# Block kernels of a state-space layer: eight 128 KB loads in place of sixteen 64 KB loads, for three of four blocks

## The chip, the cores and the metric

The kernel runs on one core of a Trainium2 chip. The metric is the device time of one execution in microseconds (us). Three runs of the kernel before are shown, and their median counts. One further execution was profiled; its trace is what all readings below come from.

## The reference

Two decoder layers over 512 positions of width 1024. The first layer mixes tokens with a diagonal complex state-space model (64 groups of 16 channels, 64 states each), followed by a GELU, a gated linear unit and an output projection; the second with stick-breaking attention. Each is followed by a layer norm and a dense SwiGLU network with its own norm. The change lies in the state-space mixer alone:

```python
mag = jnp.exp(lam_re * dt)
lbar_re = mag * jnp.cos(lam_im * dt)
lbar_im = mag * jnp.sin(lam_im * dt)
...
_, _, s_re, s_im = lax.associative_scan(
    _ssm_combine, (a_seq_re, a_seq_im, bu_re, bu_im), axis=0)
y = (jnp.einsum('lbgp,ghp->blgh', s_re, c_re.astype(f32))
     - jnp.einsum('lbgp,ghp->blgh', s_im, c_im.astype(f32)))
y = y.reshape(bsz, seq, D_MODEL) + d_skip.astype(f32) * x.astype(f32)
h = jax.nn.gelu(y).astype(x.dtype)
```

## The kernel before

The scan is not run position by position. The 512 positions are cut into 64 chunks of 8. Inside a chunk the output is a small convolution of the chunk's inputs with a kernel of lags (the intra-chunk kernel); between chunks only the states are scanned, and their effect is added. The 64 groups are handled in four blocks of 16 groups (numbered 0 to 3).

For each block the order of the work is written out by hand in `SSM_ORDER`, a string of words of one letter and a block number (or a count): `g`, `j` and `h`, `i` build tables on DVE; `t`, `T`, `m`, `M` transpose and multiply on PE; `k` (function `p_k`) computes the intra-chunk kernels on PE, ACT copies them to SBUF (L887), and two transfers of 128 KB write them to a DRAM scratch `kd` (L888); `n` (`f_n`) loads them back in another layout (L901); `r` and `s` scan the states on DVE; `y` (`p_y`, L969) is the product that needs the loaded kernels and the states; `z` transposes its result and applies the GELU; `u` is a piece of the gated linear unit on PE, `p` and `q` split a weight into two parts, `d` are products whose result isn't used. This whole stage runs under a manual schedule of all five engines, so each engine and the queues of SP and ACT execute in exactly this order.

The round trip through DRAM is needed because `p_y` wants, for each group, a 128 by 128 matrix in which partition n*16+h holds row h of the kernel shifted by n positions: the loads read `kd` eight times with overlapping windows, one load for each n, and so write 16 partitions each. In the kernel before each n is loaded twice, for groups 0 to 7 and for groups 8 to 15 of the block. The target is `tn`, two halves of 1024 columns. Blocks 0, 1 and 2 put it into idle parts of `xl` and `xh` (table `TNX`), where the two halves lie side by side, so the profile names those loads `xl<-kd` and `xh<-kd`; block 3 takes two separate tiles (`tn<-kd`). All loads are issued by SP, save the second half of block 0, which ACT issues.

`p_y` goes through 8 steps j; in each, for two groups, one product with `tn` and two with the states. Steps 0 to 3 read the first half of `tn` and steps 4 to 7 the second.

Every transfer signals one of eight completion semaphores in turn (`DMAHW0` to `DMAHW7`), so the issue of a transfer waits until the one eight places before it has landed.

Of the kernel before, what the change touches and what calls it, by code (L numbers as in the profile page):

```python
# [22 lines left out]
L = 8  # L23
# [286 lines left out]
class Trunk:  # L310
# [341 lines left out]
    def ssm(self):  # L652


        tc, nc, io, ring, ws = self.tc, self.nc, self.io, self.ring, self.ws
# [27 lines left out]
        half = lambda t, i: t[:, i * NG * L:(i + 1) * NG * L].rearrange("p (a g n) -> p a g n", a=2, n=4)  # L683
# [24 lines left out]
        for hf in range(4):  # L708
# [4 lines left out]
        kd = dr.tile([NBLK, 16, 32, 240], F32, name="kd")  # L713
# [4 lines left out]
                          in_=zero.unsqueeze(1).to_broadcast([128, NBLK * 4, 112]))  # L718
# [172 lines left out]
            ring.put(ksb)  # L891

        def f_n(b):
            if b in TNX:
                half = (self.xl, self.xh)[TNX[b]][:, 4:8].rearrange("p k t -> p (k t)").bitcast(F32)
                tn = [half[:, :1024], half[:, 1024:]]
            else:
                tn = [ring.get("tn", F32) for _ in range(2)]
            for hf in range(2):
                for n in range(L):  # L900
                    (nc.scalar if b == 0 and hf else nc.sync).dma_start(  # L901
                        out=tn[hf][n * 16:(n + 1) * 16].rearrange("p (g t) -> p g t", g=8),
                        in_=kd[b, hf * 8:hf * 8 + 8, 0:16, n * 16:n * 16 + 128].rearrange("g h t -> h g t"))
            st[b]["tn"] = tn

        def f_e(b):
# [87 lines left out]
        def f_l(b, e=V):  # L994
            tt(self.xl[:, 2 * b:2 * b + 2], st[b]["hg2"], self.xh[:, 2 * b:2 * b + 2].bitcast(F32), SUB, e)
            ring.put(st[b]["hg"])
# [61 lines left out]
        def pump(e):  # L1058
# [4 lines left out]
        fs = dict(c=a_c, g=f_g, j=lambda b: f_g(b, 1), h=f_h, i=lambda b: f_h(b, 1), d=p_d, t=p_t,  # L1063
                  T=lambda b: p_t(b, 1), m=p_m, M=lambda b: p_m(b, 1), e=f_e, k=p_k, r=f_r, y=p_y, l=f_l,
                  L=lambda b: f_l(b, G_), n=f_n, s=f_s, z=p_z,
                  B=lambda b: (powers(rest_), G_.memset(scr[0][:, 0:1], 0.0), scr_done()), b=lambda b: (levels(rest_), scr_done()))
        ET = mybir.EngineType
# [376 lines left out]
```

## Time and profile before

| | |
|---|---|
| runs | 1207.26, 1207.07, 1202.6 us; median 1207.07 us |
| profiled execution | 1201.96 us, span 1200.2 us |
| loads of blocks 0, 1, 2, 3, first issue | 34.78, 71.76, 97.92, 125.13 us |
| busy in the span: PE, DVE, ACT, POOL | 96%, 74%, 43%, 32% |
| data moved | 117.91 MB |

Times in the rows are microseconds from the start of the span. PE multiplies (PEld loads its weights), DVE, ACT and POOL are the elementwise engines, SPq and ACTq the issue of transfers on SP and ACT. "To landing" is the time from a transfer's issue to its completion signal. A row of the timeline gives start, duration, engine, line, operation, and in brackets the idle time before it and what ended it. A row by windows gives for each engine the busy time, then PE's granted clock, the busy share of the 16 DMA engines, and GB/s.

### The profile page before, as it was taken

The numbers are of one execution on the slowest core, as the hardware profiler recorded it, in microseconds if no ns is written. First come the engines' busy times: TensorE is split into PE (matmuls) and PEld (weight loads), VectorE is DVE, ScalarE is ACT, GpSimd is POOL, SyncE is SP. The second block draws the span as 40 slices with busy tenths as digits, with TensorE's granted clock in tenths as the row PEclk, the third lists the DMA queues.
The fourth block names the chain that finished last, engine by engine and source line by source line (L and its number), as shares of the span: only waits on it lengthen the run. The fifth ranks groups of instructions, "written<-read, shape, count | busy, mean of one in ns | idle before, by whom it ended". The sixth has DMA issues, their size and how long they took to land.

```text
span 1200.2 us, 20813 instructions
## 1 busy us (share of the span) xinstructions
PE 1156.9 (96%) x8494; PEld 1035.8 (86%) x8494; DVE 894.0 (74%) x1406; ACT 512.5 (43%) x813; POOL 378.6 (32%) x333
## 2 busy tenths in 40 slices
PE   3899999999999999999999999999999999999996
PEld 3777788899999999888887888878999999998885
DVE  8888585798788777435867787877987778884446
ACT  1355273054444445331156665653444444454300
POOL 6644402036455551001312322221254556510000
PEclk9999999999999999999999999999999999999999
DMA  5433741023323325431201121221233232264201
GB/s 199 115 81 81 233 168 47 1 89 108 122 87 121 109 90 197 137 110 66 106 13 59 54 71 53 72 88 53 89 106 123 72 123 90 88 227 141 70 18 52
DMA packets 44799, 117.91 MB, mean 98 GB/s; under 512 B 6816, under 2 KB 18080, under 8 KB 44576
## 3 DMA queue, kind: packets, MB, share of 16 engines
q1 hardware_dynamic: 43552, 116.07, 28.9%
q8 instruction: 66, 1.08, 0.4%
q10 hardware_dynamic: 1152, 0.52, 0.3%
q14 instruction: 29, 0.24, 0.1%
HBM read 112.51 MB, written 4.06 MB: 97 GB/s over the span
## 4 chain that ended last, share of the span: by engine, by line
PE 83%; DVE 10%; ACT 2%; issue 2%; POOL 2%; DMA 1%; SPq 0%; DVEq 0%; POOLq 0%; ACTq 0%
PE psum L359 16%; PE psum L361 16%; PE psum L360 16%; PE psum L378 8%; PE psum L380 8%; PE psum L379 8%; PE psum L969 2%; DVE nb L1212 1%; PE psum L1234 1%; ACT wh L290 1%; DVE wl L295 1%; PE psum L1299 1%; PE psum L1250 1%; POOL be L1213 1%; PE psum L1249 1%
## 5 line engine op out<-in xcount | busy, mean ns | idle before, releaser
L233 POOL TENSOR_TENSOR wf<-raw,wf 128x1024 fp32r<-128x1024 f32 (+1 forms) x80 | 160.0, 2015 | 128.5 <-ACT wf L246 81.6
L360 PE MATMUL psum<-xf,wf 128*128 128x256 f32 x640 | 181.4, 283 | 0.6 <-DVE wf L233 0.6
L361 PE MATMUL psum<-xf,wf 128*128 128x256 f32 x640 | 181.7, 284 | 0.0
L359 PE MATMUL psum<-xf,wf 128*128 128x256 f32 x640 | 181.5, 284 | 0.0
L295 DVE TENSOR_TENSOR wl<-raw,wh 128x1024 fp32r<-128x1024 f32 x91 | 119.6, 1325 | 59.1 <-ACT wh L290 40.3
L359 PE MATMUL psum<-xh,wh 128*128 128x512 f32 (+1 forms) x416 | 146.0, 352 | 1.8 <-ACT xh L992 1.3
L290 ACT ACTIVATE wh<-raw 128x1024 fp32r<-128x1024 f32 x108 | 112.4, 1054 | 76.1 <-PE psum L380 25.9
L361 PE MATMUL psum<-xl,wh 128*128 128x512 f32 (+1 forms) x416 | 141.4, 343 | 0.5 <-DVE xl L658 0.5
L360 PE MATMUL psum<-xh,wl 128*128 128x512 f32 (+1 forms) x416 | 141.1, 340 | 0.3 <-POOL wl L295 0.3
L380 PE MATMUL psum<-wh,hid 128*128 128x512 f32 x352 | 137.8, 392 | 0.0
L379 PE MATMUL psum<-wl,hid 128*128 128x512 f32 x352 | 137.5, 391 | 0.0
L378 PE MATMUL psum<-wh,hid 128*128 128x512 f32 x352 | 137.4, 390 | 0.0
L359 PE MATMUL psum<-xh,wf 128*128 128x256 f32 x480 | 134.9, 281 | 0.1
L361 PE MATMUL psum<-xl,wf 128*128 128x256 f32 x480 | 134.1, 279 | 0.0
L360 PE MATMUL psum<-xh,wf 128*128 128x256 f32 x480 | 134.1, 279 | 0.0
L360 PEld LDWEIGHTS psum<-xf,wf 128*128 128x128 f32 x640 | 122.3, 191 | 0.8 <-DVE wf L233 0.8
L359 PEld LDWEIGHTS psum<-xf,wf 128*128 128x128 f32 x640 | 122.6, 192 | 0.0
L361 PEld LDWEIGHTS psum<-xf,wf 128*128 128x128 f32 x640 | 122.3, 191 | 0.0
L295 POOL TENSOR_TENSOR wl<-raw,wh 128x1024 fp32r<-128x1024 f32 x17 | 41.9, 2476 | 177.0 <-DVE wl L295 96.6
L462 DVE TENSOR_TENSOR cv<-cv,psum 128x512 f32<-128x512 f32 x80 | 54.6, 683 | 48.6 <-PE psum L361 39.6
L359 PEld LDWEIGHTS psum<-xh,wf 128*128 128x128 f32 x480 | 90.5, 188 | 0.3 <-DVE hid L597 0.3
L361 PEld LDWEIGHTS psum<-xl,wf 128*128 128x128 f32 x480 | 90.3, 188 | 0.0
(227 smaller groups left out, 2679.2 us busy)
## 6 DMA issues: line engine op xcount, KB each, us to landing
raw<-w_gu SPq DMA_DIRECT2D x88, 512.0 KB, 3.4
raw<-w_down SPq DMA_DIRECT2D x44, 512.0 KB, 3.9
raw<-w_glu SPq DMA_DIRECT2D x16, 512.0 KB, 5.0
raw<-w_qk SPq DMA_DIRECT2D x16, 512.0 KB, 3.3
raw<-w_out SPq DMA_DIRECT2D x8, 512.0 KB, 3.4
raw<-w_v SPq DMA_DIRECT2D x8, 512.0 KB, 3.5
raw<-w_o SPq DMA_DIRECT2D x8, 512.0 KB, 3.2
xres<-xs SPq DMA_DIRECT2D x4, 512.0 KB, 6.9
```

The lines of the kernel that those rows point to most:

```text
L233: tt = lambda o, a, b, op=SUB, e=V: e.tensor_tensor(out=o, in0=a, in1=b, op=op)
L290: nc.scalar.activation(h, w, AF.Copy)
L295: (self.l_eng or nc.vector).tensor_tensor(out=l, in0=w, in1=h.bitcast(F32), op=SUB)
L359: mm(out=out, lhsT=sh, rhs=mh, start=first, stop=False)
L360: mm(out=out, lhsT=sl, rhs=mh, start=False, stop=False)
L361: mm(out=out, lhsT=sh, rhs=ml, start=False, stop=last)
L378: mm(out=o, lhsT=sh[:, ts], rhs=hl[0][:, c], start=first, stop=False)
L379: mm(out=o, lhsT=sh[:, ts], rhs=hl[1][:, c], start=False, stop=False)
L380: mm(out=o, lhsT=sl[:, ts], rhs=hl[0][:, c], start=False, stop=last)
L462: tt = lambda o, a, b, op=ADD: V.tensor_tensor(out=o, in0=a, in1=b, op=op)
L969: nc.tensor.matmul(out=yp[rows, j], lhsT=a, rhs=m_, start=step == 0, stop=step == 2)
L1212: V.tensor_tensor_scan(nb[:, h], nb[:, h], dm[u], 0.0, MUL, ADD)
```

## The change

For blocks 0, 1 and 2 one load for each n now brings all 16 groups, 16 by 16 by 128 elements (128 KB) where it was 16 by 8 by 128 (64 KB). The bytes, the 512-byte runs that they are read in, and the addresses that they go to are the same. In block 0 ACT issues the odd n and SP the even ones; before, ACT issued the second half of the groups. Block 3 keeps its 16 loads of 64 KB. The code around it moves down by four lines (L969 becomes L973), and nothing else differs.

```diff
         def f_n(b):
+
+            lags = lambda gs, n: kd[b, gs, 0:16, n * 16:n * 16 + 128].rearrange("g h t -> h g t")
             if b in TNX:
                 half = (self.xl, self.xh)[TNX[b]][:, 4:8].rearrange("p k t -> p (k t)").bitcast(F32)
                 tn = [half[:, :1024], half[:, 1024:]]
+                for n in range(L):
+                    (nc.scalar if b == 0 and n % 2 else nc.sync).dma_start(
+                        out=half[n * 16:(n + 1) * 16].rearrange("p (g t) -> p g t", g=16), in_=lags(slice(0, 16), n))
             else:
                 tn = [ring.get("tn", F32) for _ in range(2)]
-            for hf in range(2):
-                for n in range(L):
-                    (nc.scalar if b == 0 and hf else nc.sync).dma_start(
-                        out=tn[hf][n * 16:(n + 1) * 16].rearrange("p (g t) -> p g t", g=8),
-                        in_=kd[b, hf * 8:hf * 8 + 8, 0:16, n * 16:n * 16 + 128].rearrange("g h t -> h g t"))
+                for hf in range(2):
+                    for n in range(L):
+                        nc.sync.dma_start(out=tn[hf][n * 16:(n + 1) * 16].rearrange("p (g t) -> p g t", g=8),
+                                          in_=lags(slice(hf * 8, hf * 8 + 8), n))
             st[b]["tn"] = tn
```

What it does to the waits is seen in SP's queue at block 1. Before, the two writes of the kernels to `kd` stand ahead of the loads; the first load waits for the first write (`DMAHW2`), and the loads wait one after another for those eight places ahead:

```order
L888 DMA kd<-ksb_754 128x2x128 [waits DMAHW2_49,Activation_49]
L888 DMA kd<-ksb_754 128x2x128 [waits DMAHW3_49,Activation_49]
L901 DMA xh<-kd 16x8x128 [waits DMAHW4_49,DMAHW2_49]
L901 DMA xh<-kd 16x8x128 [waits DMAHW5_49]
L901 DMA xh<-kd 16x8x128 [waits DMAHW6_49]
L901 DMA xh<-kd 16x8x128 [waits DMAHW7_49]
L901 DMA xh<-kd 16x8x128 [waits DMAHW0_49]
L901 DMA xh<-kd 16x8x128 [waits DMAHW1_49]
L901 DMA xh<-kd 16x8x128
L901 DMA xh<-kd 16x8x128 [waits DMAHW3_49]
```

(eight more loads follow). With the change:

```order
L888 DMA kd<-ksb_746 128x2x128 [waits DMAHW2_49,Activation_49]
L888 DMA kd<-ksb_746 128x2x128 [waits DMAHW3_49,Activation_49]
L900 DMA xh<-kd 16x16x128 [waits DMAHW4_49,DMAHW3_49,DMAHW2_49]
L900 DMA xh<-kd 16x16x128 [waits DMAHW5_49]
L900 DMA xh<-kd 16x16x128 [waits DMAHW6_49]
L900 DMA xh<-kd 16x16x128 [waits DMAHW7_49]
L900 DMA xh<-kd 16x16x128 [waits DMAHW0_49]
L900 DMA xh<-kd 16x16x128 [waits DMAHW1_49]
L900 DMA xh<-kd 16x16x128 x2
L226 DMA raw_843<-w_glu 128x1024 [waits DMAHW4_49,PE_49]
```

The first load now waits for both writes (`DMAHW2` and `DMAHW3`), and no load waits for another load of its block.

On PE, at the middle of block 1's `p_y` (from the end of step 2 to step 4), the kernel before waits for the eight loads of the second half:

```order
L969 MATMUL psum<-h_736,s_923 64x128 x2
L969 MATMUL psum<-xh,xres 64x128 x2
L969 MATMUL psum<-h_701,s_923 64x128 x2
L969 MATMUL psum<-h_736,s_923 64x128 x2
L969 MATMUL psum<-xh,xres 64x128 [waits DMAHW4_49,DMAHW3_49,DMAHW5_49,DMAHW2_49,DMAHW6_49,DMAHW1_49,DMAHW7_49,DMAHW0_49,Activation_49]
```

With the change only a wait for ACT is left there, and the first product of `p_y` waits for all eight loads of the block, so for both halves:

```order
L973 MATMUL psum<-h_728,s_907 64x128 x2
L973 MATMUL psum<-xh,xres 64x128 x2
L973 MATMUL psum<-h_693,s_907 64x128 x2
L973 MATMUL psum<-h_728,s_907 64x128 x2
L973 MATMUL psum<-xh,xres 64x128 [waits Activation_49]
```

## The prediction

> **What bounds the kernel now.** I read the page first: the busy shares and the shares of the chain that ended last.
>
> ```profile
> PE 1156.9 (96%) x8494; PEld 1035.8 (86%) x8494; DVE 894.0 (74%) x1406; ACT 512.5 (43%) x813; POOL 378.6 (32%) x333
> PE 83%; DVE 10%; ACT 2%; issue 2%; POOL 2%; DMA 1%; SPq 0%; DVEq 0%; POOLq 0%; ACTq 0%
> ```
>
> PE bounds the whole, and DMA holds 1% of the chain. So a load is worth something only where PE stands still for it, or where a later load would make PE stand still. Next come PE's waits up to 180 us, where the loads of the four blocks lie (total, times, longest).
>
> ```profile
> PE psum L969 <- DMA tn<-kd: 1.4, 1, 1.4
> PE psum L969 <- DMA xl<-kd: 1.2, 1, 1.2
> PE psum L969 <- issue: 0.2, 1, 0.2
> ```
>
> Two waits for these loads exist: 1.4 us for `tn` in block 3, which the change leaves as it is, and 1.2 us for `xl`. The timeline of SP and ACT shows the loads of blocks 0, 1 and 2 (start, duration), that of PE the products that use them.
>
> ```profile
> 32.84 0.89 SPq L888 DMA_DIRECT2D kd<-ksb  x2
> 34.78 5.44 SPq L901 DMA_DIRECT2D xl<-kd  x8
> 35.29 6.17 ACTq L901 DMA_DIRECT2D xl<-kd  x8
> 69.06 1.78 SPq L888 DMA_DIRECT2D kd<-ksb  x2
> 71.76 7.42 SPq L901 DMA_DIRECT2D xh<-kd  x16
> 95.00 1.75 SPq L888 DMA_DIRECT2D kd<-ksb  x2
> 97.92 7.67 SPq L901 DMA_DIRECT2D xl<-kd  x16
> ```
>
> ```profile
> 43.80 0.44 PE L969 MATMUL psum<-xl,xres 128*64 128x128 f32 x4 [1.15 <-DMA xl<-kd]
> 52.89 1.06 PE L834 MATMUL psum<-ident,g 128*128 128x128 f32 x8 [0.37 <-DVE g L658]
> 53.79 1.04 PE L984 MATMUL psum<-ident,ysb 128*128 128x128 f32 x8
> 77.78 0.44 PE L969 MATMUL psum<-xh,xres 128*64 128x128 f32 x4 [0.18 <-issue]
> 81.67 0.44 PE L969 MATMUL psum<-xh,xres 128*64 128x128 f32 x4
> 105.68 0.44 PE L969 MATMUL psum<-xl,xres 128*64 128x128 f32 x4
> 109.50 0.44 PE L969 MATMUL psum<-xl,xres 128*64 128x128 f32 x4
> ```
>
> The reader is to see how close this is. Block 0's product starts at 43.80 after waiting 1.15 us for its loads. Block 1's starts at 77.78 with no wait for a load; its second half, steps 4 to 7, starts at 81.67. Block 2's starts at 105.68, its second half at 109.50. The prices of single transfers come from the view of the tile `kd`, cut to one or a few issues (duration of the issue, first and last start; then issue to landing, minimum, median, maximum): block 1's loads, then the second write of `kd` in blocks 1, 2 and 0.
>
> ```profile
> L901 SPq DMA_DIRECT2D xh<-kd x16: 325/429/430, 71.8 to 78.8; - x16
> DMA to landing us min/median/max: 2.2/2.4/2.5
> L888 SPq DMA_DIRECT2D kd<-ksb x1: 1315/1315/1315, 69.5 to 69.5; - x1
> DMA to landing us min/median/max: 2.8/2.8/2.8
> L888 SPq DMA_DIRECT2D kd<-ksb x1: 1282/1282/1282, 95.5 to 95.5; - x1
> DMA to landing us min/median/max: 2.8/2.8/2.8
> L888 SPq DMA_DIRECT2D kd<-ksb x1: 414/414/414, 33.3 to 33.3; - x1
> DMA to landing us min/median/max: 1.9/1.9/1.9
> ```
>
> Block 1's sixteen loads are issued 7.42/16 = 0.464 us apart and each lands 2.4 us after its issue. The eighth, issued at 71.76 + 7 x 0.464 = 75.0, lands at 77.4: 0.4 us before PE uses the first half at 77.78. The sixteenth, issued at 78.8, lands at 81.2, 0.5 us before 81.67. The two halves arrive just in time.
>
> What limits the loads is read from windows (the last two columns are the busy share of the DMA engines and GB/s):
>
> ```profile
> 36.00:41.00 5.00, 5.00 (x47) 5.00 (x46) 4.92 (x12) 0.00 (x0) 4.04 (x10) 1.00 1.05 166
> 73.00:78.00 5.00, 4.82 (x25) 3.65 (x23) 4.96 (x5) 2.16 (x4) 5.00 (x5) 1.00 0.61 137
> 99.00:105.00 6.00, 6.00 (x28) 4.94 (x27) 5.11 (x6) 2.76 (x5) 6.00 (x6) 1.00 0.66 137
> ```
>
> In blocks 1 and 2 the DMA engines are only 0.61 and 0.66 busy while SP issues one load after another with an issue time of 0.429 us: there the issue sets the pace, at 137 GB/s. In block 0, where SP and ACT issue together, the engines are full (1.05) and move 166 GB/s.
>
> **The change part by part.** Per block sixteen loads become eight of twice the size. It removes 8 issues; it keeps all bytes (8 x 128 KB = 1.05 MB) and the 512-byte runs. The page's queue row for ACT shows how a load is cut:
>
> ```profile
> q10 hardware_dynamic: 1152, 0.52, 0.3%
> ```
>
> 1152 packets for 8 loads of 64 KB are 144 each: 128 runs of 512 bytes and 16 more. So only those 16 are saved per removed load, 11% of the packets, and the work of the DMA engines stays. [...]
>
> Two things are added. First, a load reads all 16 groups, so it waits for the second write to `kd` as well. Second, the first product of `p_y` waits for the whole 1.05 MB, where it waited for 0.52 MB.
>
> When the eight loads land isn't in the trace; I bound it. Below: the issue still paces, 0.464 us each, and a 128 KB load lands like the 64 KB load (2.4) or like the 128 KB write (2.8). Above: the engines pace. A lone load of 64 KB takes 2.4 us, of which 0.48 is its data at 137 GB/s, so 1.9 us are fixed; to these comes 1.05 MB at some rate. If 0.61 busy at 137 GB/s scales, the full rate is 225 GB/s (4.7 us). Block 0's mixture measured 166 (6.3 us). I take 200 GB/s (5.2 us), between the two: block 0 is the only row of full engines, but two queues with waits between their loads stand in it, which hold it down.
>
> Block 1. The second write is issued at 69.53 and lands 2.8 later, at 72.3: the loads start 0.5 us later than now. Issue-paced the last one goes out at 72.3 + 7 x 0.464 = 75.6 and lands at 78.0 to 78.4, so PE starts 0.2 to 0.6 late. Engine-paced: 72.3 + 1.9 + 4.7, 5.2 or 6.3 = 78.9, 79.4 or 80.5, so 1.1, **1.6** or 2.7 us late. The second half, before due at 81.67, then has no wait, but it had none before.
>
> Block 2. Loads start at 95.5 + 2.8 = 98.3; issue-paced they land by 104.4, engine-paced at 104.9, 105.4 or 106.5. PE needs them at 105.68: **0**, above 0.8 us. A shift from block 1 moves both sides alike, since the kernels of block 2 come from PE too.
>
> Block 0. Both queues start at 33.3 + 1.9 = 35.2; the data lands at 35.2 + 1.9 + 4.7, 5.2 or 6.3 = 41.8, 42.3 or 43.4. All are before 43.80, so PE's wait of 1.15 us shrinks or goes. It is worth **0**: PE's next stop is at 52.89 for DVE's table `g`, which doesn't depend on this product, and the result's transposes (53.79) stand behind it in order. If that cover failed, the gain would be at most 1.15. ACT's four issues fewer are hidden too, since its next work waits 11.88 us for DVE; and what SP loads next are weights of products after 58 us, none of which waits for a transfer in the list of waits above.
>
> ```profile
> 44.97 0.28 ACT L803 ACTIVATE psum<-pk 128x128 f32<-128x128 f32 x1 [11.88 <-DVE pk L658]
> ```
>
> Does block 1's delay reach the end? DVE is behind PE there, not ahead:
>
> ```profile
> 90.96 1.22 DVE L658 TENSOR_TENSOR w<-e,psum 128x1024 f32<-128x1024 f32 x1 [4.32 <-PE psum L845]
> 94.17 0.38 PE L879 MATMUL psum<-h,g 64*32 64x112 f32 x4 [0.93 <-issue]
> ```
>
> DVE idles 4.32 us for PE at 90.96, and PE's own stop of 0.93 us at 94.17 follows a burst of small products and moves with it. So nothing takes the delay up, and it arrives whole. Sum: 0 + 1.6 + 0 = **+1.6 us** on the profiled execution's 1201.96 (span 1200.2 and 1.8 around it), so 1203.6; bounds without another mechanism +0.2 and +3.5 (2.7 + 0.8).
>
> **The rivals.** (a) The issue stays the pace also at twice the size, all three blocks land in time but for 0.2 to 0.6 us: 1202.4. For it: engines 0.61 busy; against: twice the bytes at the same spacing would be 1.22 busy. [...] (b) Faster: block 0's wait of 1.15 us goes and the gain passes on, with block 1 in time: 1200.8. Against it stands DVE's table at 52.89. (c) Slower: the 137 GB/s aren't the issue's pace but that of eight rows of 16 partitions, each load reaching 16 partitions only; then 1.05 MB takes 7.7 us. Block 1 lands at 72.3 + 1.9 + 7.7 = 81.9, 4.1 late; block 2 at 107.9, 2.2 late; block 0 at 44.8, 1.0 late, of which the 0.37 at 52.89 takes up some: 0.6. Together +6.9: 1208.9 on the profiled execution, 0.57%. It decides from a rate below about 145 GB/s. Against it: block 0 reached 166 with the same shapes.
>
> **How the numbers follow.** Chances: forecast (0.8 to 3.5 us slower) 0.65, (a) 0.17, (b) 0.07, (c) 0.08, none of these 0.03. What a measurement can tell from no change is about 0.5%, 6.0 us; of these cases only (c) reaches it. But the shown executions themselves lie apart: 1201.96 and 1202.6 against 1207.07 and 1207.26. Added to the median, the forecast gives 1208.7; added to the mean of the four (1204.7) it gives 1206.3; I take **1207.0**, since either level may hold the median after. The range runs from 1202.6 - 1.15 = 1201.4 to 1207.26 + 3.5 = 1210.8, rounded to 1201 and 1211. Within 0.5%: 0.85; slower 0.08 from (c); faster 0.07, from a median on the lower level with (b) or more.
>
> **What would show it.** In the changed profile: eight issues of `xh<-kd` starting near 72.3, not 71.8; DMA busy share near 1 from 74 to 79 us; landings growing from 2.5 to 4 us; a wait of 1 to 2.7 us of the product on `xh<-kd` (none before), with no load wait of the product in block 2; block 0's wait under 1.15 us and the stop for `g` grown by what it lost. The prediction is wrong if block 1's product starts by 77.9 (then (a)), if the work after 58 us comes earlier than before (then (b)), or if loads stay at 137 GB/s with full queues (then (c)).

## The result and the profile after

The changed kernel takes 1218.84 us (median of four executions, 1217.28 to 1220.06) against 1205.86 for the kernel before (median of four, 1202.6 to 1207.26), a ratio of 1.0121 (95% interval 1.0105 to 1.0137; the quotient of the two medians, 1.0108, lies within it). It is 1.2% slower. The forecast was 1207.0 us, between 1201 and 1211, and no change within 0.5%. All ratios here leave out one execution of 1900.94 us at a granted clock of 0.56, one of ten of the kernel with the change in block 0 alone. The profiled execution has a span of 1215.5 us against 1200.2: 15.3 us more.

The page of the changed kernel, its first row and the chain that ended last:

```profile
PE 1162.7 (96%) x8494; PEld 1038.6 (85%) x8494; DVE 894.8 (74%) x1406; ACT 512.2 (42%) x813; POOL 380.3 (31%) x333
PE 82%; DVE 10%; DMA 3%; ACT 2%; issue 1%; POOL 1%; SPq 1%; DVEq 0%; POOLq 0%; ACTq 0%
```

PE is busy 5.8 us longer with the same number of instructions, and DMA has 3% of the chain where it had 1%. Nearly all of the loss is found in the first 150 us. First SP's transfers (start, duration), then PE's products that use them, of the changed kernel:

```profile
69.04 1.57 SPq L888 DMA_DIRECT2D kd<-ksb  x2
72.16 3.76 SPq L900 DMA_DIRECT2D xh<-kd  x8
103.26 1.81 SPq L888 DMA_DIRECT2D kd<-ksb  x2
106.62 3.76 SPq L900 DMA_DIRECT2D xl<-kd  x8
137.31 1.69 SPq L888 DMA_DIRECT2D kd<-ksb  x2
```

```profile
43.63 0.44 PE L973 MATMUL psum<-xl,xres 128*64 128x128 f32 x4 [1.07 <-DMA raw<-w_glu]
82.74 0.69 PE L973 MATMUL psum<-xh,xres 128*64 128x128 f32 x4 [5.21 <-issue]
89.44 0.44 PE L973 MATMUL psum<-xh,xres 128*64 128x128 f32 x4
117.36 0.69 PE L973 MATMUL psum<-xl,xres 128*64 128x128 f32 x4 [3.35 <-DMA xl<-kd]
123.83 0.44 PE L973 MATMUL psum<-xl,xres 128*64 128x128 f32 x4
147.16 0.44 PE L973 MATMUL psum<-tn,xres 128*64 128x128 f32 x4 [1.84 <-DMA tn<-kd]
```

Up to 69 us nothing has moved (the first write of block 1's kernels stands at 69.04, before at 69.06). Then the ledger runs so. Block 1's product starts at 82.74, before at 77.78: 5.0 us. Its first four steps take 82.74 to 89.44 = 6.7 us, before 77.78 to 81.67 = 3.9: 2.8 us more, in the same instructions. Block 2's product waits 3.35 us, and its first four steps take 6.5 us, before 3.8: 2.7 more. Block 3's wait, for loads that the change doesn't touch, is 0.46 longer (1.84 against 1.38). Together 14.3 of the 15.3; what is left comes in pieces under 1 us.

The wait of 5.21 at 82.74 carries no name, but the landings of block 1's loads give it: the last of the eight is issued at 75.5 and lands 6.9 later, at 82.4.

```profile
L900 SPq DMA_DIRECT2D xh<-kd x8: 324/446/448, 72.2 to 75.5; - x8
DMA to landing us min/median/max: 3.1/5.1/6.9
```

The slow first halves are PE's clock. By windows (the third column from the right is the granted clock, then the busy share of the DMA engines, which can come out above 1, and GB/s):

```profile
74.00:80.00 6.00, 3.54 (x16) 2.57 (x14) 5.93 (x6) 2.77 (x5) 6.00 (x6) 1.00 1.24 132
83.00:89.00 6.00, 6.00 (x46) 3.69 (x46) 3.55 (x4) 0.00 (x0) 0.00 (x0) 0.50 0.17 66
108.00:116.00 8.00, 6.01 (x27) 4.60 (x25) 7.07 (x8) 2.68 (x5) 5.42 (x5) 1.00 1.23 139
117.00:123.00 6.00, 5.64 (x40) 3.36 (x40) 5.97 (x6) 0.00 (x0) 0.00 (x0) 0.50 0.31 123
```

From just before the end of the wait the granted clock is 0.50, for 6.8 us in block 1 (82.6 to 89.4) and again in block 2. And the loads move at 132 GB/s with the DMA engines' share at 1.24, where the sixteen small loads moved 137 GB/s at 0.61.

### The profile page after: what moved, and what is told of

Read it like the earlier page. It is cut to its first block, busy times and chain, and to the rows that moved or that the text cites. A ratio compares the mean times of both kernels' runs of the same rounds, so it can differ in the third digit from the quotient of the medians.

```text
span 1215.5 us, 20778 instructions
## 1 busy us (share of the span) xinstructions
PE 1162.7 (96%) x8494; PEld 1038.6 (85%) x8494; DVE 894.8 (74%) x1406; ACT 512.2 (42%) x813; POOL 380.3 (31%) x333
## 4 chain that ended last, share of the span: by engine, by line
PE 82%; DVE 10%; DMA 3%; ACT 2%; issue 1%; POOL 1%; SPq 1%; DVEq 0%; POOLq 0%; ACTq 0%
PE psum L359 15%; PE psum L361 15%; PE psum L360 15%; PE psum L378 8%; PE psum L380 8%; PE psum L379 8%; PE psum L973 2%; DVE nb L1216 1%; PE psum L1238 1%; ACT wh L290 1%; DVE wl L295 1%; PE psum L1303 1%; PE psum L1254 1%; PE psum L879 1%; POOL be L1217 1%
## 5 line engine op out<-in xcount | busy, mean ns | idle before, releaser
L359 PEld LDWEIGHTS psum<-xh,wf 128*128 128x128 f32 x480 | 90.4, 188 | 0.3 <-DVE hid L597 0.3
L360 PEld LDWEIGHTS psum<-xh,wf 128*128 128x128 f32 x480 | 90.2, 188 | 0.0
```

Source lines behind the costliest of these rows:

```text
L359: mm(out=out, lhsT=sh, rhs=mh, start=first, stop=False)
L360: mm(out=out, lhsT=sl, rhs=mh, start=False, stop=False)
```

## The experiments

The theory after the result: (1) eight loads in turn to 16 neighbouring partitions each are paced by their destination; (2) PE must have the whole block first; (3) the two waits cost PE its clock. Rivals for the pace are the source (rows 30 KB apart in DRAM) and the size of a transfer; for the clock, that it falls with the transfers whatever PE does.

**Dummy products in the waits.** On the changed kernel, in the written order (each `d` is a number of products whose result isn't used):

```diff
-e2 s1 g2 y1 ...  u1 u1 s2 y2
+e2 s1 g2 d9 d9 d4 y1 ...  u1 u1 s2 d9 d5 y2
```

> The changed kernel with dummy products added on PE in front of the intra-chunk product of block 1 (22 instructions of 0.23 us, 5.0 us) and of block 2 (14, 3.2 us), which fill most of the time that PE waits there for the loads; nothing else is changed. If half of the loss is the lower clock that PE is granted after those two waits (0.50 for some 6 us each), the clock stays at 1.0, the first half of both products takes 3.9 us again in place of 6.7 and 6.5, and the span falls by 5.0 to 6.0 us from 1215.5, to about 1210. If the clock would fall whatever PE does there (by the amount of transfers, say), the span stays within 1 us of 1215.5.

Measured: ratio to the kernel before 1.0067 (1.0045 to 1.0089), 0.54% or 6.5 us less than the changed kernel's (3 to 10 us by the two intervals). The clock stays at 1.00 at blocks 1 and 2; block 1's rows:

```profile
78.00:84.00 6.00, 5.31 (x34) 4.44 (x33) 5.93 (x6) 2.73 (x4) 6.00 (x6) 1.00 1.26 114
86.87 0.44 PE L973 MATMUL psum<-xh,xres 128*64 128x128 f32 x4
90.69 0.44 PE L973 MATMUL psum<-xh,xres 128*64 128x128 f32 x4
45.00:48.00 3.00, 3.00 (x26) 1.68 (x24) 2.49 (x3) 2.32 (x4) 1.50 (x1) 0.50 1.02 406
62.00:65.00 3.00, 3.00 (x9) 2.35 (x8) 2.96 (x4) 0.60 (x1) 0.00 (x0) 0.50 0.00 0
```

The four steps take 3.8 us again (86.87 to 90.69), with the DMA engines as full as before (1.26, in the changed kernel 1.24). So the clock follows PE's idle time here, and it costs 0.54% of the 1.21% that the change loses; the ledger's 2.8 and 2.7 us say much the same. This span, 1211.6, is 3.9 us under the changed kernel's and not 5 to 6, since in this execution the clock fell in block 0 as well, at 45 and at 62 (last two rows), after waits of 1.8 and 1.3 us. Two falls of 3.4 us at half clock make some 3.4 us, an estimate from these rows.

**Destination or source.** Two runs on the changed kernel, each with one side of the load altered; rows land in the wrong partitions in the one and are the wrong rows in the other, all else is the same.

```diff
-out=half[n * 16:(n + 1) * 16].rearrange("p (g t) -> p g t", g=16), in_=lags(slice(0, 16), n))
+out=half[n::8].rearrange("p (g t) -> p g t", g=16), in_=lags(slice(0, 16), n))
```

> The changed kernel, but load n writes partitions n, n+8, ..., n+120 in place of 16n to 16n+15, so that the rows of the kernels land in other partitions (the output isn't the reference's). Same sources, sizes, queues and waits. If the pace of 128 GB/s with the DMA engines over 1.2 busy comes from eight transfers in turn each writing 16 neighbouring partitions, the rate in block 1 rises to 200 GB/s or more, the last load lands before 79.5 us, the wait at block 1's product falls from 5.2 us to under 2, and block 2's from 3.35 to under 0.8; span 1204 or less. If the source in DRAM or the issue of 256 runs per load sets the pace, rate and waits stay: 125 to 140 GB/s, 5 us, span 1215.

```diff
-in_=lags(slice(0, 16), n))
+in_=kd[b, 0:1, 0:16, n * 16:n * 16 + 128].to_broadcast([16, 16, 128]).rearrange("g h t -> h g t"))
```

> The changed kernel, but each load reads the rows of its first group 16 times in place of 16 groups that lie 30 KB apart in DRAM (the output isn't the reference's). Destinations, sizes, queues and waits are the same. If the spread of the source sets the pace of 128 GB/s, the rate rises over 180 GB/s and the wait at block 1's product falls under 2.5 us. If it is the destination, or the number of runs, the rate stays at 125 to 140 GB/s and the wait at about 5 us, span about 1215.

A window of six microseconds while block 1's loads run, and the loads' issue and landing, first with the spread destination, then with the narrow source:

```profile
76.00:82.00 6.00, 3.84 (x17) 2.82 (x15) 5.97 (x6) 3.08 (x5) 6.00 (x7) 1.00 0.91 201
L900 SPq DMA_DIRECT2D xh<-kd x8: 543/607/609, 74.4 to 78.9; - x8
DMA to landing us min/median/max: 3.0/3.9/4.2
```

```profile
78.00:84.00 6.00, 3.35 (x15) 2.43 (x13) 5.96 (x6) 2.73 (x4) 6.00 (x6) 1.00 1.26 113
L900 SPq DMA_DIRECT2D xh<-kd x8: 325/446/454, 75.3 to 78.6; - x8
```

With the destination spread over partitions 8 apart the rate rises from 132 to 201 GB/s at a share of 0.91. With the source narrowed it doesn't rise (113; on the same chip the unaltered loads in the run with dummy products moved 114). At block 2, too, the spread destination has 198 to 200 GB/s in each microsecond from 108 to 111. So the destination sets the pace here. The 201 are no limit of the spread destination: a load of 128 KB is issued every 0.64 us there (74.4 to 78.9), and that allows 204. Between 201 and 113, on one chip, lies a factor of 1.8; why 16 neighbouring partitions took so much less, no run shows.

The time was not as expected for the spread destination: a span of 1210.7 (one execution) and not 1204 or less, since PE still waited 3.7 us at block 1, where under 2 was expected. The issue of such a load takes 0.607 us, not 0.446, so the last is issued at 78.9 and lands 4.2 later, at 83.1. Why the issue is longer was not tried. At block 2, whose loads have more time, the wait fell to 0.94 us, from 3.35 in the changed kernel and 3.18 with the narrow source. With the narrow source the span is 1218.7 (one execution).

**Size or order.** The sixteen 64 KB loads of before, issued lag by lag, both halves of the groups in turn:

```diff
-    (nc.scalar if b == 0 and n % 2 else nc.sync).dma_start(
-        out=half[n * 16:(n + 1) * 16]..., in_=lags(slice(0, 16), n))
+    for hf in range(2):
+        (nc.scalar if b == 0 and n % 2 else nc.sync).dma_start(
+            out=tn[hf][n * 16:(n + 1) * 16]..., in_=lags(slice(hf * 8, hf * 8 + 8), n))
```

> Sixteen loads of 64 KB as before, but issued lag by lag (first and second half of the groups for n = 0, then for n = 1, and so on), so the first product of a block needs all sixteen, as in the changed kernel, and only the size differs. If needing the whole block first is most of the loss, the loads keep their pace of 0.46 us and 2.4 us to landing, the last one lands near 81.1, the wait at block 1's product is 3.2 to 3.6 us (5.2 in the changed kernel), block 2's about 1.8 (3.35), and a lower clock follows the first: span 1207 to 1212. If the loss comes from the size of the transfers, there is no wait over 1 us and the span is that of the kernel before, 1200 to 1202.

```profile
74.00:78.00 4.00, 4.00 (x19) 3.27 (x18) 3.93 (x5) 1.77 (x3) 4.00 (x4) 1.00 0.62 134
79.00:82.00 3.00, 0.00 (x0) 0.00 (x0) 2.97 (x4) 1.34 (x2) 2.95 (x4) 1.00 1.27 105
84.06 0.70 PE L975 MATMUL psum<-xh,xres 128*64 128x128 f32 x4 [5.29 <-DMA xh<-kd]
```

The wait is 5.29, nearly that of the changed kernel (5.21), and the time 1217.3 (one execution). Neither expectation held in full: the loads don't keep their pace. They start at 134 GB/s with the engines 0.62 busy, and from 79 us on they are at 105 and 1.27. By then two 64 KB loads in turn to the same 16 partitions behave like one of 128 KB (132 at 1.24), so it is not the size of a transfer here; it is which partitions follow each other.

**Needing the whole block, at the old rate.** The kernel before, its loads untouched, with the products of blocks 1 and 2 taking their second half first:

```diff
-for j in range(GB):
+for j in ((4, 5, 6, 7, 0, 1, 2, 3) if b in (1, 2) else range(GB)):
```

> The kernel before, its loads untouched, but the products of blocks 1 and 2 take their steps 4 to 7 first, so the first product needs the half that is loaded last, and with it all sixteen loads, at the old pace. This prices needing the whole block apart from the rate. From the trace of before: the last load of block 1 lands at 78.8 + 2.4 = 81.2, so PE waits 3.4 us from 77.8 (5.2 in the changed kernel); block 2's lands at 107.5, a wait of 1.8 (3.35). If both are followed by a lower clock, 1.5 to 3 us each come on top: span 1208 to 1211. If the rate were the whole of the changed kernel's loss, these waits would be under 1 us.

```profile
73.00:79.00 6.00, 5.02 (x22) 3.77 (x21) 5.93 (x6) 2.91 (x6) 6.00 (x6) 1.00 0.54 123
82.60 0.70 PE L969 MATMUL psum<-xh,xres 128*64 128x128 f32 x4 [4.58 <-DMA xh<-kd]
115.62 0.59 PE L969 MATMUL psum<-xl,xres 128*64 128x128 f32 x4 [2.09 <-DMA xl<-kd]
```

Ratio 1.0076 (1.0059 to 1.0093); the median of 1211.85 us is a span of some 1210, as expected. The trace is that of the slowest of the four executions (1216.26), in which the clock also fell once at block 3. The loads run as before (engines 0.54 busy, 2.5 us to landing), and still PE waits 4.58 and 2.09 us (3.4 and 1.8 were expected), followed by a clock of 0.50 both times. Part of the 4.58 is that the loads are first issued at 72.66 in this execution, 0.9 later than before. So waiting for the whole block alone makes most of the two waits, and the merge gives nothing back: from the first issue to the product it is 9.9 us with the sixteen small loads and 10.6 with the eight big ones (72.16 to 82.74).

**Two queues.** The odd lags by ACT in all three blocks:

```diff
-(nc.scalar if b == 0 and n % 2 else nc.sync).dma_start(
+(nc.scalar if n % 2 else nc.sync).dma_start(
```

> The changed kernel with the odd n issued by ACT in blocks 1 and 2 too, so that at any time loads to two groups of 16 partitions are under way. If the destination's 16 partitions set the pace, two queues lift it from 128 to 170 to 220 GB/s (block 0 of the changed kernel moved 174 to 268), the eight loads land by 79.5, and the wait at block 1's product falls from 5.2 to under 2 us. ACT pays 4 us at each block for waiting on the writes and issuing, which may hold back its copies out of PSUM and with them PE by 1 to 3 us. Span 1204 to 1209. If the engines or the source set the pace, it stays at 128 and the span at 1215 or more.

```profile
78.00:83.00 5.00, 3.35 (x9) 2.68 (x10) 4.97 (x5) 2.41 (x4) 3.75 (x3) 0.66 1.28 188
79.65 0.80 PE L359 MATMUL psum<-xh,wh 128*128 128x512 f32 x1 [3.46 <-ACT part L1025]
```

Ratio 1.0098 (1.0076 to 1.012), slower than expected. The window has 188 GB/s, but part of it is a weight load that SP issues at 79.95, and how much the loads themselves gained isn't shown. ACT stands at its issues until the writes to `kd` have landed (it is without other work for 4.74 us in block 1 and 5.07 in block 2), its copies out of PSUM come late, and PE waits 3.46 and 3.43 us for them; the clock falls there instead. It neither shows nor refutes the pace by destination, and it is no way out.

**One block alone.** The 128 KB loads in one block, all others loaded as before:

```diff
-if b in TNX:
+if b in TNX and b != 1:      # the sixteen loads of the kernel before
+    ...
+elif b in TNX:
```

> Only block 1 has the 128 KB loads; blocks 0, 2 and 3 are loaded as before. If each block's loss stands by itself, block 1's start is 5.0 us late and the lower clock after it costs 2.8: span 1200.2 + 7.8 = 1208 (between 1207 and 1209.5), with block 2's product starting without a wait. If the loss is one of the whole (a slower stage after the first change, or a clock that falls in blocks 0 and 2 too), the span is over 1211.

> Only block 2 has the 128 KB loads. By the changed kernel's trace it costs 3.35 us of waiting and 2.9 of lower clock: span 1200.2 + 6.3 = 1206.5 (between 1205 and 1208). If blocks 1 and 2 only lose together, under 1203.

> Only block 0 has the 128 KB loads, odd n issued by ACT. In the changed kernel's trace its product started 0.17 us earlier than before and all later work up to 69 us was in place: span 1200 to 1202. In other runs with these loads PE waited 1.8 to 2.4 us there and its clock fell to 0.50 twice, and the work at 69 us was 3.4 late: then the median is 2 to 4 us (0.2 to 0.3%) above before. By the sum of the single blocks (0.54% and 0.62% against 1.21%) it is about 0.05%.

Block 1 alone: ratio 1.0054 (1.0037 to 1.0071), span 1207.6, a wait of 6.0, and none at block 2. Block 2 alone: 1.0062 (1.0041 to 1.0083), span 1207.0, a wait of 3.4. Both spans lie where they were expected. Block 0 alone: 0.9999 (0.9985 to 1.0013), by its times alone. The sum of the three, 1.15%, is the changed kernel's 1.21% within the intervals: blocks 1 and 2 lose by themselves, and block 0, whose first product was already waiting, shows neither a gain nor a loss beyond 0.15%.

**Versions to beat the kernel before.** Three runs on it: block 3's loads ahead of a weight load in SP's queue, eight dummy products in block 0's idle places, and both (the last is shown).

```diff
-k0 n0 d9 r0 d9 d9 d9 d9 s0 ... z0 m1 M1 h1 l0 ... i3 k3 p n3 u1
+k0 n0 d9 r0 d9 d9 d9 d9 d4 s0 ... z0 m1 M1 d4 h1 l0 ... i3 k3 n3 p u1
```

> The kernel before with one thing changed: in the written order of block 3 its loads stand ahead of the next weight load in SP's queue (n3 before p). Before, the 512 KB weight load runs ahead of them and they land in 3.2 us at the median, not 2.4, and PE waits 1.4 us for them. If that weight load is what delays them, the wait falls to 0.2 us or less and the time by 1.2 us (0.1%); if it doesn't matter, the wait stays and so does the time. If the weight is missed later, the time rises by up to 2 us.

> The kernel before with eight dummy products more on PE (0.9 us each four): four ahead of block 0's product, where PE waits 0.4 to 1.7 us for the loads, and four behind block 0's transposes, where it waits 1.3 us for ACT. In several of the runs with spans over 1202 PE's clock is granted at 0.50 for 3.3 us from about 45 or 60, after these two waits. If that is what spreads the times of the kernel before, the profile shows 1.00 throughout the first 150 us, the time lies at 1200 to 1203 in nearly all executions and the median falls by 1 to 2 us. If the spread comes from elsewhere, the median is the same or up to 1 us later.

> The same, and block 3's loads ahead of the weight load in SP's queue. If the weight load ahead costs PE some of its 1.4 us at block 3, this is 0.3 to 1.2 us faster than the one with dummy products alone; otherwise the same.

Block 3's loads first: 0.9992 (0.998 to 1.0004); the loads land in 2.5 us at the median, 3.2 before, but PE's wait is still 1.1 us, where 0.2 or less was expected. In its profile the clock fell at block 0:

```profile
60.00:62.00 2.00, 2.00 (x6) 1.53 (x5) 1.97 (x3) 0.60 (x1) 0.00 (x0) 0.50 0.00 0
```

Dummy products alone: 1.0004 (0.9994 to 1.0013), with the clock lost later in its profile, at 70 and at 135 us after waits of 1.7 and 2.2, and times from 1201.2 to 1205.54 (1201.1 to 1207.77 for the kernel before on that chip); that expectation failed. Both together: 1200.41 us, 0.9983 (0.9975 to 0.9992), and in its profile the clock is 1.00 throughout and block 3's wait 0.40:

```profile
40.00:72.00 32.00, 27.96 (x412) 21.89 (x412) 28.87 (x38) 15.75 (x25) 14.92 (x13) 1.00 0.28 88
72.00:140.00 68.00, 66.00 (x903) 50.32 (x902) 53.94 (x49) 32.47 (x49) 32.70 (x22) 1.00 0.43 123
129.76 0.44 PE L969 MATMUL psum<-tn,xres 128*64 128x128 f32 x4 [0.40 <-DMA tn<-kd]
```

It is the fastest version found, 0.17% under the kernel before and 1.4% under the changed one. Against the dummy products alone it gains some 2.5 us, more than the 0.3 to 1.2 expected; the clock that wasn't lost is the likely rest, which no run separates.

## Why the prediction was wrong

- **Where the loads start, and their issue: right.** They start at 72.16 (72.3 forecast), held back by the second write, and are issued 0.47 us apart.
- **The rate of the loads: wrong, and this is the step that failed first.** The prediction's "I take 200 GB/s" measured 132 in block 1 and 139 in block 2. Two inferences led there. The busy share of 0.61 at 137 GB/s was scaled to 225 at full; but the share was no measure of room here: at 1.24 the engines moved 132 GB/s, at 0.61 they moved 137. And block 0's 166 GB/s was read as a floor and as evidence against rival (c), although there two queues wrote at once. With the spread destination 201 were measured, so 200 was possible; to 16 neighbouring partitions each, from one queue, it was 132 and 139.
- **Block 1: 5.0 us late, not 1.6; block 2: 3.35 of waiting, not 0.** With the whole block needed and nothing gained in rate, both follow; rival (c) had them at 4.1 and 2.2 with chance 0.08, and it is the rival that came nearest. It came near partly by luck: its 137 GB/s was the pace of the small loads, one per 0.464 us and each landed 2.4 us later, and the big loads happened to run near it. Its sum of 6.9 us is less than half of the loss, for it has no clock either.
- **Block 0 at nothing: right.** The product started 0.17 earlier, the stop for `g` took 0.48 us where it took 0.37, and PE's work at 69 us was where it had been; alone, the block gives 0.9999.
- **The delay arrives whole: right, and more than whole.** What was missing from the sum is the clock. After the two waits PE ran at 0.50 for 6.8 us each, 2.8 and 2.7 us by the ledger, 6.5 us by the dummy products. The working took a delay as a shift, and so put this term at nothing without a reason. Among the loads' waits the trace of before gave no hint (1.38 us at block 3 without a fall in the clock). But it has one long wait, 18.8 us ahead of PE's first product, and the products behind it are slow:

```profile
18.80 1.94 PE L834 MATMUL psum<-ident,g 128*128 128x128 f32 x8 [18.80 <-DVE g L658]
20.53 4.05 PE L852 MATMUL psum<-ident 128*128 128x128 f32 x18
26.55 2.28 PE L852 MATMUL psum<-ident 128*128 128x128 f32 x18
```

The same 18 products take 4.05 us at 20.53 and 2.28 at 26.55, though the clock column shows 1.00 for both. So slow products behind a long wait could be read before the change, and their price should have stood among the bounds.

- **Of the forecast signs**, the start near 72.3, the engines full from 74 on and no gain at block 0 came true; landings grew to 6.9 and not 4, block 1 waited 5.21 and not 1 to 2.7, and block 2 did wait.
- **The scatter of the runs**, from which the middle of the forecast was taken, has the clock as a likely part: executions of several kernels show one or two falls of 3.4 us at block 0 and others none. That it explains the spread of the kernel before was only argued. The two levels that the forecast saw in it don't show in the 65 later executions: these run from 1200.85 to 1208.05 and fill the range between, and their medians on four chips are 1202.0 to 1203.4.

What stays open is why sixteen loads in the old order hold 137 GB/s at 0.61 busy while loads that stay twice as long on the same partitions fall to 105 to 139, and whether it goes by how many sets of partitions are under way; and the longer issue of the load with a spread destination, and with it how fast that destination could be written.

## What to carry to other kernels

Merging transfers gained nothing here, although the small ones had gone out one issue behind the other (0.464 us apart, the DMA engines 0.61 busy): the rate was 137 GB/s before, 132 and 139 after. Look first at which partitions each one writes (on one chip 113 GB/s to 16 neighbours, 201 to 16 that lie 8 apart), and at whether the next in the queue writes others (two in turn to the same 16 went from 134 GB/s down to 105). An order of loads that lets the consumer start on half the data was worth more here than fewer loads: needing the whole block alone cost 0.76%. Price a wait on PE with the clock that follows it, since the waits of 5.21 and 3.35 us here cost some 5.5 to 6.5 us more after they had ended.

## What the runs showed of the hardware

- 128 KB loads to 16 neighbouring partitions, in a queue: 113 to 139 GB/s at 1.23 to 1.26 busy; the same bytes to 16 partitions 8 apart: 201 GB/s at 0.91, about what their issue allows.
- In thirteen traces (all runs but block 0 alone), from PE's first product to 150 us, each fall of PE's granted clock to 0.50 lasts 3.4 or 6.8 us. Twelve waits of 3.18 us or more all brought one: nine of them 6.8 us (after 3.18 to 6.04 us of waiting), three 3.4 us (after 3.43, 3.46 and 3.69). So the length of the wait alone didn't set the price.
- Shorter waits brought a fall of 3.4 us in some executions and none in others. A wait of 1.67 us at 69 us brought one in the run with the dummy products alone, and none in the run with block 3's loads moved as well; waits of 1.3 and 0.5 us a microsecond apart brought one at 62 us in the run with dummy products in the waits, and none in the profiles of the kernel before and of the changed one.
